# Bias tables without their zero columns and a landing margin for row products, in a one-core hybrid attention and state-space kernel

## The chip, the core and the metric

The kernel runs on one core of one Trainium2 chip. Its time is the device time of one execution in microseconds (us); lower is better. The time of a kernel is the median over several executions, and one further execution was recorded by the profiler. The engines are TensorE (PE; its weight loads are listed as PEld), VectorE (DVE), ScalarE (ACT), GpSimd (POOL) and SyncE (SP), which here only issues DMAs.

## The reference

Two layers are computed over 256 latent tokens (`x`, width 2048) with 256 context tokens. Each layer first makes a shift, a scale and a gate row from a conditioning vector by a vector-matrix product (`adaln`), normalizes and modulates the tokens, and adds the gated result of its mixer:

```python
for i in range(DEPTH):                      # 2 layers
    shift, scale, gate = adaln(c, ada_w[i], ada_b[i])     # silu(c) @ w + b, in three
    h = modulate(rms_norm(x, norm_g[i]), shift[:, None], scale[:, None])
    ...
    y = na_ssd_mixer(...) if i % 2 == 0 else short_conv_mixer(...)
    x = x + gate[:, None] * y
```

The first mixer has 16 neighbourhood-attention heads of width 128 and 32 state-space (SSD) heads behind one input projection, the second a gated short convolution. In an attention head the scores between the 256 latent queries (4 rows of 64) and the 256 latent keys get a bias that depends on the difference of row and column, and a mask that leaves 16 columns per query:

```python
bias = rpb[:, dr_idx[None, :, None], dc_idx[:, None, :]].reshape(nh, GRID_W, kh * GRID_W)
s_lat = jnp.einsum('bqhd,bkhd->bhqk', qr, kb).astype(jnp.float32) * scale + bias.astype(jnp.float32)
s_lat = jnp.where(mask, s_lat, -jnp.inf)
```

All is float32, and every large product is formed from three matmuls of split operands, described next.

## The kernel before

**Weights.** Each large weight comes from DRAM as pieces of 128 x 1024 floats (512 KB) into one of five buffers `raw` (L381 and L383, issued by SP). ACT rounds a piece to a short float (L420, the high half), DVE subtracts this from the piece (L427, the low half), and the two halves stand in one of three places `w0`, `w1`, `w2`. TensorE then forms high x high, high x low and low x high (L195). L427 is called a split below. A `raw` buffer is free again, and the next load into it can be issued, once its split has run. When three places are in use, a split waits until TensorE is done with the oldest.

**Stages.** After a start that makes the first layer's modulation, TensorE does the input projection for each of four groups of heads (to about 1100 us), then the output projection in three passes of columns, and then the second layer. Attention heads (`head_gen`) and SSD groups (`group_gen`) are done on DVE, ACT and TensorE beside the projections.

**What sets the order.** The work is written as generators in three queues: `urgent`, `side` (heads and groups) and `back`. A generator yields the engine it wants next, the tiles that must be ready, and how many PSUM banks it needs. A planner (class `Plan`) keeps a clock for each engine and for each tile, moved on by rough costs that are written in the kernel. The function `may` (L241) decides whether the next piece of a task is written now. For SP it asks that the tiles are ready by the planner's clock; for DVE and ACT that the engine's clock is within a horizon of TensorE's clock (`hor`: 4500, 2500 and 1500 ns for the three queues) and that the tiles are ready at most 400 ns from now. Once written, an instruction stands in its engine's queue for good: if its data comes later than planned, the engine waits there, and all that stands behind waits too.

**Row products.** The gate rows and the second layer's modulation need 2048 x 8192 weights (`adaT`). They are not multiplied by TensorE: the one task in `back` (`gemv_gen`) loads 128 pieces of 512 KB through the same `raw` buffers (L381) and multiplies and sums each on DVE with a broadcast row `csb` (L823, named CUSTOM_DVE_ANT_0 in the profile and ISA in the order of instructions). Results are first needed in the output projection, then in the second layer.

**Bias tables.** Two tiles `bias0` and `bias1` take turns over the 16 heads. For each head SP loads one table of 128 x 672 floats (336 KB, L1073) after the head two before has finished, DVE adds the mask in three places (L1078: columns 0 to 128, 304 to 368 and 544 to 672), and L1096 adds the table to the scores of each query half. The columns between are a gap of zeros that the table in DRAM holds.

**Other DVE work** named below: L1480 and L1483 scale an SSD group's output, L942 and L1613 make the low half of a mixed row, L1140 that of the attention weights, L571 and L989 normalize keys; L1456, L1461 and L1162 belong to SSD groups and heads.

Of the kernel before, what the change touches and what calls it, by code (L numbers as in the profile page):

```python
# [141 lines left out]
def kernel(ctx: ExitStack, tc, x, cx, ada0, w0, adaT, w_in, w_out, sc_in, sc_out, rpb, small, const,  # L142
# [7 lines left out]
    V, S, G, T, DMA = nc.vector, nc.scalar, nc.gpsimd, nc.tensor, nc.sync  # L150
    DMA2 = nc.scalar
    plan = Plan()
    E = plan.add

    def st(shape, tag, dt=F32, name=None):
        return sb.tile(list(shape), dt, tag=tag, name=name or tag, bufs=1)

    def drt(shape, name):
        return dr.tile(list(shape), F32, name="dram_" + name)
# [79 lines left out]
    def grow(task):  # L239
        _, t, h = task.cond  # L240
        if t - task.tmps > budget[0] or h - task.halves > budget[1]:  # L241
            return False
        cap(task, t, h)
        return True

    def may(task, hor, isurg):
        eng, aps, nb = task.cond
        if eng == "if":
            return aps()
        if eng == "grow":  # L250
            return grow(task)
        if nb and len(free_b) < nb + (0 if isurg else reserve[0]):
            return False
        if eng == "DVE":
            lows_try()
        now, t = plan.t["PE"], plan.t["ACT" if eng == "AQ" else eng]
        rdy = plan.ready(aps)
        if eng == "AQ":
            return t <= now + hor and rdy <= t
        if hor < 2000 and nb and sorted(plan.last[b.tensor.name] for b in free_b)[nb - 1] + 3000 > now:  # L260
            return False
        if hor < 2000:
            rdy += 4000 if eng == "PE" else 0
        if eng == "PE":
            if nb:
                rdy = max(rdy, sorted(plan.last[b.tensor.name] for b in free_b)[nb - 1])
            return rdy + (0 if isurg else 800) <= now + 100
        if eng == "SP":
            return rdy <= max(t, now) + 200
        return t <= now + hor and rdy <= max(t, now) + 400  # L270
# [7 lines left out]
    def pump():  # L278
        splits_try()
        again = True  # L280
        while again:
            again = False
            for q, hor in HOR[:2] if hold[0] else HOR:
                for task in list(q):
                    if not begin(task):
                        continue
                    if task.cond == "end":
                        sweep(q)
                        continue
                    if may(task, hor, q is urgent):  # L290
                        run(q, task)
                        if task.cond == "end":
                            sweep(q)
                        again = True
                        break
                if again:
                    break
# [134 lines left out]
    def lows_try():  # L432
        while lows and not hold[0] and plan.ready([lows[0][1]]) <= max(plan.t["PE"], plan.t["DVE"]) + 200:
            low_part()
# [340 lines left out]
    bias = [st([128, 3, 256], f"bias{k}") for k in range(2)]  # L775
# [149 lines left out]


    vd = drt([256, 512], "vd")
    dcol = P_("dcol")


# [136 lines left out]
    def head_gen(a, h):  # L1067
        hd = 4 * a + h
# [1 line left out]
        yield when(lambda: hd < 2 or ("pv", hd - 2) in got)  # L1070
        yield W_("SP")
        bf = bt.rearrange("p a b -> p (a b)")[:, :672]
        E(DMA.dma_start(bf, rpb[hd]))  # L1073
        yield W_("DVE", bt)
        for o_, m_ in ((0, mask[:, 0:32]), (304, mid), (544, mask[:, 32:64])):
            n_ = m_.shape[-1]
# [475 lines left out]
    for h in range(4):  # L1552
        spawn(side, head_gen(0, h))
# [11 lines left out]
    def do_qk(a, nxt):  # L1565
        psQ = banks(2)
        proj(512, "act", psQ, 4)
        spawn(urgent, kq_gen("Q", a, psQ, 2, statq, QT, QL, True), 2)
        psK = banks(4)
        proj(512, "act", psK, nxt)  # L1570
        spawn(urgent, kq_gen("K", a, psK, 4, statk, KT, KL, True), 4)
        for h in range(4 if a < 3 else 0):
            spawn(side, head_gen(a, h))
# [19 lines left out]
    for h in range(4):  # L1593
        spawn(side, head_gen(3, h))
# [516 lines left out]
```

## Time and profile before

| what | value |
|---|---|
| three timed executions | 1760.16, 1758.64, 1757.49 us (median 1758.64) |
| the profiled execution | 1761.34 us |
| its span, first to last instruction | 1759.6 us |
| PE busy / DVE busy / ACT busy / POOL busy | 1733.2 / 1218.6 / 768.1 / 31.4 us |
| mean granted TensorE clock | 0.999 |
| DMA | 381.86 MB, mean 217 GB/s |

In lines of groups the columns are: source line, engine, operation, tiles as out<-in with shapes, count, then busy time and the mean of one in ns, then the idle time of the engine just before such an instruction and what ended it. In lines of waits: how long in total, how many times, the longest. In rows of the timeline: start and duration in us, engine, line, and in brackets the idle time before and what released the instruction. In rows by stretch: the stretch, its length, each engine's busy time with its count, the granted clock, the share of DMA and GB/s.

### The profile page before, as it was taken

To read this page: it belongs to the slowest core of one execution; us is meant where nothing else is said; L and a number is where in the kernel's file an instruction comes from. 1 tells how busy PE (TensorE), PEld (TensorE's weight loads), DVE (VectorE), ACT (ScalarE), POOL (GpSimd) and SP (SyncE) were. 2 spreads that over 40 slices of the span, in tenths; PEclk is the share of its full clock that TensorE was granted. 3 is DMA by queue.
4 is the path that set the end of the run, shared out by engine and by line. 5 is a ranking of instruction groups with operands and counts; after the bars stand their busy time and mean duration, and the time that the engine had idled before them with its cause. 6 is when DMAs were issued, how large, how long until landed. Compare 5 with 4: busy or idle time off the path is not lost.

```text
span 1759.6 us, 25036 instructions
## 1 busy us (share of the span) xinstructions
PE 1733.2 (99%) x9451; PEld 1462.6 (83%) x9451; DVE 1218.6 (69%) x2042; ACT 768.1 (44%) x1330; POOL 31.4 (2%) x26
## 2 busy tenths in 40 slices
PE   6999999999999999999999999999999999999998
PEld 4777989888888888888888898888888888888887
DVE  5666777878476868676878687887668555555554
ACT  5333544446243436243436343664445444444432
POOL 0000100000000001000000000000000000000000
PEclk9999999999999999999999999999999999999999
DMA  9977644685765766665677567767867666666563
GB/s 368 347 295 258 206 150 150 201 241 190 231 198 158 239 190 209 207 220 171 212 219 219 180 213 239 242 227 266 290 218 251 208 187 192 191 191 191 190 205 120
DMA packets 188761, 381.86 MB, mean 217 GB/s; under 512 B 15536, under 2 KB 51168, under 8 KB 188640
## 3 DMA queue, kind: packets, MB, share of 16 engines
q1 hardware_dynamic: 181376, 373.68, 65.4%
q10 hardware_dynamic: 7264, 6.58, 1.1%
q8 instruction: 74, 1.21, 0.3%
q14 instruction: 47, 0.39, 0.1%
HBM read 372.71 MB, written 7.50 MB: 216 GB/s over the span
## 4 chain that ended last, share of the span: by engine, by line
PE 94%; DMA 2%; DVE 2%; ACT 1%; issue 0%; SPq 0%; POOL 0%; DVEq 0%; ACTq 0%
PE bank L195 90%; PE bank L199 3%; DMA tmp<-dram_csr 1%; DVE w L427 1%; DMA raw<-in_adaT 1%; DMA raw<-in_ada 0%; DVE raw L823 0%; DMA bias<-in_rpb 0%; ACT w L420 0%; DVE tmp L1456 0%; ACT tmp L1441 0%; DVE tmp L1445 0%; SPq L583 0%; ACT tmp L1451 0%; DVE tmp L759 0%
## 5 line engine op out<-in xcount | busy, mean ns | idle before, releaser
L420 ACT CAST w<-raw 128x1024 fp32r<-128x1024 f32 x343 | 359.1, 1049 | 519.9 <-PE bank L195 443.6
L427 DVE TENSOR_TENSOR w<-raw,w 128x1024 fp32r<-128x1024 f32 x343 | 416.5, 1218 | 232.9 <-ACT w L420 223.6
L195 PE MATMUL bank<-hH,w 128*128 128x256 f32 (+1 forms) x2064 | 488.4, 325 | 5.4 <-DVE w L427 5.4
L195 PE MATMUL bank<-w,hH 128*128 128x512 f32 x1280 | 406.3, 395 | 2.7 <-ACT hH L757 2.5
L195 PEld LDWEIGHTS bank<-hH,w 128*128 128x128 f32 x2064 | 345.7, 189 | 38.4 <-DVE w L427 6.6
L195 PE MATMUL bank<-hL,w 128*128 128x256 f32 (+1 forms) x1040 | 335.0, 322 | 0.0
L195 PEld LDWEIGHTS bank<-w,hH 128*128 128x128 f32 x1280 | 236.8, 188 | 54.1 <-issue 3.9
L195 PE MATMUL bank<-w,hL 128*128 128x512 f32 x640 | 249.5, 390 | 0.1
L195 PEld LDWEIGHTS bank<-hL,w 128*128 128x128 f32 x1040 | 197.0, 189 | 14.4
L195 PE MATMUL bank<-w,h 128*128 128x512 f32 x768 | 179.7, 390 | 0.0
L823 DVE CUSTOM_DVE_ANT_0 raw<-raw,csb 128x1024 f32<-128x1024 f32 x128 | 155.6, 1220 | 28.7 <-DMA raw<-in_adaT 23.0
L195 PEld LDWEIGHTS bank<-w,h 128*128 128x128 f32 x768 | 143.6, 188 | 29.6
L195 PEld LDWEIGHTS bank<-w,hL 128*128 128x128 f32 x640 | 120.1, 188 | 25.5 <-DVE hL L763 0.6
L195 PE MATMUL bank<-w,mix 128*128 128x512 f32 x588 | 138.6, 392 | 0.8 <-DVE w L427 0.8
L195 PEld LDWEIGHTS bank<-w,mix 128*128 128x128 f32 x588 | 109.3, 188 | 23.5 <-DVE w L427 1.7
L1276 DVE SCALAR_TENSOR_TENSOR tmp<-bank,cwh,tmp 128x508 f32<-128x508 f32 (+1 forms) x96 | 71.2, 745 | 1.8
L195 PE MATMUL bank<-KL,h 128*128 128x512 f32 x264 | 63.8, 389 | 0.0
L427 DVE TENSOR_TENSOR KL<-raw,KL 128x1024 fp32r<-128x1024 f32 x32 | 39.2, 1224 | 32.4 <-ACT KL L420 32.4
L427 DVE TENSOR_TENSOR QL<-raw,QT 128x1024 fp32r<-128x1024 f32 x32 | 39.2, 1224 | 29.4 <-ACT QT L420 29.3
L427 DVE TENSOR_TENSOR wL<-raw,wH 128x1024 fp32r<-128x1024 f32 x31 | 37.9, 1224 | 30.4 <-ACT wH L420 30.4
L195 PEld LDWEIGHTS bank<-KL,h 128*128 128x128 f32 x264 | 49.5, 188 | 10.2
L195 PE MATMUL bank<-QT,h 128*128 128x512 f32 x168 | 56.2, 391 | 0.0
(292 smaller groups left out, 1972.6 us busy)
## 6 DMA issues: line engine op xcount, KB each, us to landing
raw<-in_w_in SPq DMA_DIRECT2D x196, 512.0 KB, 3.8
raw<-in_adaT SPq DMA_DIRECT2D x128, 512.0 KB, 4.7
raw<-in_sc_in SPq DMA_DIRECT2D x128, 512.0 KB, 3.7
raw<-in_w_out SPq DMA_DIRECT2D x64, 512.0 KB, 4.9
raw<-in_ada SPq DMA_DIRECT2D x34, 512.0 KB, 6.7
raw<-in_sc_out SPq DMA_DIRECT2D x32, 512.0 KB, 3.6
PT<-in_ada SPq DMA_DIRECT2D x16, 512.0 KB, 6.9
raw<-in_w SPq DMA_DIRECT2D x16, 512.0 KB, 6.2
```

The source lines that it names most:

```text
L195: E(T.matmul(o, l, r, start=start, stop=stop, skip_group_check=True))
L199: E(T.transpose(o, i, ident if k == 128 else ident[:k, :k]))
L420: E(S.copy(H, v))
L427: E(V.tensor_tensor(out=Lo, in0=v, in1=H.bitcast(F32), op=ALU.subtract))
L823: E(V.tensor_tensor_reduce(out=raw, in0=raw, in1=csb, scale=1.0, scalar=0.0, op0=ALU.mult, op1=ALU.add, accum_out=gp[:, h, m:m + 1]))
L1276: E(V.scalar_tensor_tensor(out=do, in0=di, scalar=cwh[:, 32 * k + ch:32 * k + ch + 1], in1=do, op0=ALU.mult, op1=ALU.add))
```

## The change

1. The table in DRAM loses its gap: 320 columns per head in place of 672. SP loads it in three pieces (128, 64 and 128 columns: 64, 32 and 64 KB) into the same places of the tile. The zeros in between are written once, by POOL, into both tiles.
2. In `may`, a task of the queue `back` that wants DVE must have its tiles ready 2000 ns earlier by the planner's clock. Only the row products are in `back`.

```diff
@@ in may @@
         if hor < 2000:
-            rdy += 4000 if eng == "PE" else 0
+            rdy += 4000 if eng == "PE" else 2000 if eng == "DVE" else 0
@@ before the heads @@
+    for b_ in bias:
+        E(G.memset(b_.rearrange("p a b -> p (a b)")[:, 128:544], 0.0))
@@ in head_gen @@
         bf = bt.rearrange("p a b -> p (a b)")[:, :672]
-        E(DMA.dma_start(bf, rpb[hd]))
+        for o_, c_, n_ in ((0, 0, 128), (304, 128, 64), (544, 192, 128)):
+            E(DMA.dma_start(bf[:, o_:o_ + n_], rpb[hd, :, c_:c_ + n_]))
@@ in kernel(), on the host @@
-    gap = np.zeros((16, 128, 176), np.float32)
-    table = np.concatenate([pick(0, kc[:32]), gap, pick(0, kc[32:40]), pick(1, kc[24:32]), gap, pick(1, kc[32:])], axis=2)
+    table = np.concatenate([pick(0, kc[:32]), pick(0, kc[32:40]), pick(1, kc[24:32]), pick(1, kc[32:])], axis=2)
```

Lines behind the edits move by two or three: the mask's add is L1078 before and L1081 after, the table's load L1073 and L1076, and so on for all lines behind it.

Since the planner's clock decides what is written when, the order moves from the first row products on (about 170 us into the run). TensorE has the same instructions in another order; SP has 32 more DMAs, POOL two more instructions. The six row products that ran first stood ahead of the 35th split before; now 49 splits stand ahead of the sixth. The 64th stood behind 148 of DVE's 450 splits and now stands behind 162; the last behind 315, now 358. Three places follow, all on DVE.

**Place 1**, around a pair of tables whose load is issued at 402.56 us in the profile. `w0` to `w2` are weight places, `statk` belongs to the keys' norm, `half` and `yi` to an SSD group. Before:

```order
L1078 TENSOR_TENSOR bias0_159<-bias0_159,const_111 128x128
L1078 TENSOR_TENSOR bias1_160<-bias1_160,const_111 128x128
L1078 TENSOR_TENSOR bias1_160<-bias1_160,const_111 128x64
L1078 TENSOR_TENSOR bias1_160<-bias1_160,const_111 128x128
L427 TENSOR_TENSOR w2_97<-raw2_92,w2_97 128x1024
L823 ISA raw1_91,gp_167<-raw1_91,csb_166 128x1024
L823 ISA gp_167 128x1
L571 TENSOR_SCALAR statk_161<-statk_161 128x16
L1480 TENSOR_TENSOR half7_81<-bank7_89,yi_106 128x256
L1483 TENSOR_TENSOR half7_81<-half7_81,sz_104 128x256
L427 TENSOR_TENSOR w0_95<-raw0_90,w0_95 128x1024
```

Now:

```order
L1081 TENSOR_TENSOR bias0_159<-bias0_159,const_111 128x128
L1081 TENSOR_TENSOR bias1_160<-bias1_160,const_111 128x128
L1081 TENSOR_TENSOR bias1_160<-bias1_160,const_111 128x64
L1081 TENSOR_TENSOR bias1_160<-bias1_160,const_111 128x128
L823 ISA raw1_91,gp_167<-raw1_91,csb_166 128x1024
L823 ISA gp_167 128x1
L427 TENSOR_TENSOR w2_97<-raw2_92,w2_97 128x1024
L571 TENSOR_SCALAR statk_161<-statk_161 128x16
L427 TENSOR_TENSOR w0_95<-raw4_94,w0_95 128x1024
```

A row product has moved from behind the split of `w2` to ahead of it, and nothing long stands between the splits of `w2` and `w0` any more.

**Place 2**, around a later pair of tables, loaded from 669.56 us in the profile. Before:

```order
L1078 TENSOR_TENSOR bias1_160<-bias1_160,const_111 128x128
L1078 TENSOR_TENSOR bias1_160<-bias1_160,const_111 128x64
L1078 TENSOR_TENSOR bias1_160<-bias1_160,const_111 128x128
L823 ISA raw3_93,gp_167<-raw3_93,csb_166 128x1024
L823 ISA gp_167 128x1
L571 TENSOR_SCALAR statk_161<-statk_161 128x16
L427 TENSOR_TENSOR w0_95<-raw1_91,w0_95 128x1024
L427 TENSOR_TENSOR w1_96<-raw0_90,w1_96 128x1024
L427 TENSOR_TENSOR w2_97<-raw4_94,w2_97 128x1024
```

Now, from the row product ahead of the tables on:

```order
L823 ISA raw3_93,gp_167<-raw3_93,csb_166 128x1024
L823 ISA gp_167 128x1
L1081 TENSOR_TENSOR bias0_159<-bias0_159,const_111 128x128
L1081 TENSOR_TENSOR bias0_159<-bias0_159,const_111 128x64
L1081 TENSOR_TENSOR bias0_159<-bias0_159,const_111 128x128
L1081 TENSOR_TENSOR bias1_160<-bias1_160,const_111 128x128
L1081 TENSOR_TENSOR bias1_160<-bias1_160,const_111 128x64
L1081 TENSOR_TENSOR bias1_160<-bias1_160,const_111 128x128
L427 TENSOR_TENSOR w1_96<-raw4_94,w1_96 128x1024
L427 TENSOR_TENSOR w2_97<-raw2_92,w2_97 128x1024
L427 TENSOR_TENSOR w0_95<-raw1_91,w0_95 128x1024
```

Before, a split of `w1` and one of `w2` stood ahead of the tables, and a row product behind them and ahead of the next split of `w0`. Now the tables come ahead of those splits of `w1` and `w2`, a row product stands right ahead of the tables, and none between them and the split of `w0`.

**Place 3**, in the first pass of the output projection, ahead of the split that ends at about 1152.8 us in the profile; `mix` rows are the projection's other operand. Before:

```order
L823 ISA raw0_90,gp_167<-raw0_90,csb_166 128x1024
L823 ISA gp_167 128x1
L942 TENSOR_TENSOR mix12_9348<-half5_79,mix12_9348 128x256
L1140 TENSOR_TENSOR PL_2289<-bank2_84,PH_2288 128x4x128
L1140 TENSOR_TENSOR PL_2289<-bank7_89,PH_2288 128x4x128
L1613 TENSOR_TENSOR mix26_9361<-tmp2_67,mix26_9361 128x256
L427 TENSOR_TENSOR w0_95<-raw2_92,w0_95 128x1024
```

Now:

```order
L823 ISA raw2_92,gp_167<-raw2_92,csb_166 128x1024
L823 ISA gp_167 128x1
L427 TENSOR_TENSOR w0_95<-raw1_91,w0_95 128x1024
L427 TENSOR_TENSOR w1_96<-raw3_93,w1_96 128x1024
L1459 SCALAR_TENSOR_TENSOR tmp0_65<-tmp6_71,dtl_1622,tmp0_65 128x128 x2
L1464 TENSOR_TENSOR tmp3_68<-tmp0_65 128x256
L1165 TENSOR_TENSOR half2_76<-bank5_87,gt_101 128x256
L1143 TENSOR_TENSOR PL_2293<-bank4_86,PH_2292 128x4x128
```

The split of `w0` stands right behind the row product; the four instructions that stood between come later or elsewhere.

## The prediction

> **What bounds the kernel now.** The first part of the page gives each engine's busy time, and a line of its fifth part the row products:
>
> ```profile
> PE 1733.2 (99%) x9451; PEld 1462.6 (83%) x9451; DVE 1218.6 (69%) x2042; ACT 768.1 (44%) x1330; POOL 31.4 (2%) x26
> L823 DVE CUSTOM_DVE_ANT_0 raw<-raw,csb 128x1024 f32<-128x1024 f32 x128 | 155.6, 1220 | 28.7 <-DMA raw<-in_adaT 23.0
> ```
>
> PE is busy in 1733.2 of 1759.6 us and its matmuls stay the same, so whatever the change does to DVE, DMA or SP counts only where PE stands still for it. I therefore looked for PE's idle time, first by stretches:
>
> ```profile
> 0.00:38.00 38.00, 23.25 (x155) 15.64 (x156) 21.73 (x65) 23.15 (x50) 2.41 (x8) 1.00 0.96 375
> 400.00:415.00 15.00, 13.35 (x126) 12.48 (x123) 12.81 (x28) 10.86 (x43) 2.90 (x1) 1.00 0.57 186
> 660.00:705.00 45.00, 41.23 (x291) 38.25 (x291) 36.57 (x79) 26.85 (x78) 4.53 (x2) 0.96 0.64 205
> 1130.00:1180.00 50.00, 49.22 (x261) 41.06 (x260) 42.53 (x94) 29.44 (x61) 1.39 (x2) 1.00 0.71 236
> 1180.00:1754.00 574.00, 573.72 (x2590) 475.25 (x2589) 343.72 (x409) 253.96 (x311) 1.49 (x2) 1.00 0.65 210
> ```
>
> The start loses 14.75 us before any row product or table exists; the change leaves it alone but for two memsets. Between 38 and 1754 us three stretches hold the loss: 1.65, 3.77 and 0.78 us. The waits name one cause for it, and PE's timeline has the five places:
>
> ```profile
> PE bank L195 <- DVE w L427: 6.2, 5, 3.0
> 409.53 0.39 PE L195 MATMUL bank<-hH,w 128*128 128x256 f32 x1 [0.77 <-DVE w L427]
> 413.40 0.38 PE L195 MATMUL bank<-hH,w 128*128 128x256 f32 x1 [0.88 <-DVE w L427]
> 669.16 0.39 PE L195 MATMUL bank<-hH,w 128*128 128x256 f32 x1 [0.81 <-DVE w L427]
> 682.09 0.39 PE L195 MATMUL bank<-hH,w 128*128 128x256 f32 x1 [2.96 <-DVE w L427]
> 1152.85 0.50 PE L195 MATMUL bank<-w,mix 128*128 128x512 f32 x1 [0.78 <-DVE w L427]
> ```
>
> Each time a split came late: 0.77 + 0.88 + 0.81 + 2.96 + 0.78 = 6.20 us. The longest has a sequel, which the granted clock (third column from the right) shows in stretches of 2 us:
>
> ```profile
> 682.00:684.00 2.00, 1.91 (x14) 1.91 (x15) 2.00 (x3) 0.00 (x0) 2.00 (x1) 0.87 0.86 270
> 684.00:686.00 2.00, 2.00 (x12) 2.00 (x11) 1.50 (x3) 0.20 (x1) 0.79 (x1) 0.50 0.91 299
> 686.00:688.00 2.00, 2.00 (x15) 2.00 (x15) 2.00 (x4) 0.84 (x1) 0.00 (x0) 0.78 0.99 331
> 688.00:690.00 2.00, 2.00 (x20) 2.00 (x19) 1.48 (x3) 1.57 (x3) 0.00 (x0) 1.00 0.63 183
> ```
>
> After 2.96 us without work the clock fell: (0.13 + 0.50 + 0.22) x 2 = 1.70 us of work lost, though PE reads as busy. The four stalls under 0.9 us had no such sequel. The pool from which this change can gain is 6.20 + 1.70 = **7.90 us**.
>
> Why the splits were late stands in DVE's timeline:
>
> ```profile
> 406.83 0.63 DVE L1078 TENSOR_TENSOR bias<-bias,const 128x128 f32<-128x128 f32 x3 [1.11 <-DMA bias<-in_rpb]
> 407.70 0.63 DVE L1078 TENSOR_TENSOR bias<-bias,const 128x128 f32<-128x128 f32 x3 [0.24 <-DMA bias<-in_rpb]
> 408.25 1.22 DVE L427 TENSOR_TENSOR w<-raw,w 128x1024 fp32r<-128x1024 f32 x1
> 410.11 1.23 DVE L823 CUSTOM_DVE_ANT_0 raw<-raw,csb 128x1024 f32<-128x1024 f32 x1 [0.64 <-DMA raw<-in_adaT]
> ...
> 666.74 1.23 DVE L823 CUSTOM_DVE_ANT_0 raw<-raw,csb 128x1024 f32<-128x1024 f32 x1 [0.23 <-DMA raw<-in_adaT]
> ...
> 675.98 0.63 DVE L1078 TENSOR_TENSOR bias<-bias,const 128x128 f32<-128x128 f32 x3 [1.15 <-DMA bias<-in_rpb]
> 676.87 0.63 DVE L1078 TENSOR_TENSOR bias<-bias,const 128x128 f32<-128x128 f32 x3 [0.26 <-DMA bias<-in_rpb]
> 679.59 1.23 DVE L823 CUSTOM_DVE_ANT_0 raw<-raw,csb 128x1024 f32<-128x1024 f32 x1 [2.09 <-DMA raw<-in_adaT]
> 680.82 2.37 DVE L427 TENSOR_TENSOR w<-raw,w 128x1024 fp32r<-128x1024 f32 x2
> ```
>
> At 409 us the tables held DVE for 1.11 + 0.24 us right ahead of a split; at 413 and 669 us a row product stood ahead of one; at 682 us tables (1.15 + 0.26) and a row product (2.09) did so together. At 1152 us it was a row product and four short instructions.
>
> **The change part by part.** The profiled execution took 1761.34 us, 1.74 beyond its span, and lies 2.70 above the median of the timed runs, 1758.64. I add up against 1761.34 and take the 2.70 off at the end.
>
> *The margin.* In the new order a row product no longer stands between the tables and the split that was late at 682 us, none stands right ahead of the split at 669, and at 1152 the four short instructions are gone from between. These orders cover all five stalls, so the whole pool goes: **-7.90**. What takes their place is worked out next, from how the tables arrive.
>
> *The tables in three pieces.* These rows have SP's issues and how long they took to land:
>
> ```profile
> L1073 SPq DMA_DIRECT2D bias<-in_rpb x16: 422/461/944, 223.0 to 1159.8; - x16
> DMA to landing us min/median/max: 4.1/4.7/8.8
> 402.56 0.93 SPq L1073 DMA_DIRECT2D bias<-in_rpb  x2
> 662.26 1.33 SPq L1432 DMA_DIRECT2D tmp<-dram_csr  x2
> 669.56 0.94 SPq L1073 DMA_DIRECT2D bias<-in_rpb  x2
> tmp<-dram_exr SPq DMA_DIRECT2D x32, 128.0 KB, 5.3
> 673.32 0.28 PE L195 MATMUL bank<-hH,w 128*128 128x256 f32 x1
> ```
>
> A table of 336 KB lands in 4.7 us and a transfer of 128 KB in 5.3, so fewer bytes don't land sooner here; I give a piece the time t of a whole table, 4.1 to 8.8. Six issues in place of two at 0.46 us each put the last piece 4 x 0.46 = 1.85 later.
>
> Place 1: the issues stood behind the load that follows the split of w1, and stand ahead of both now, at least 1.22 + 0.37 = 1.59 sooner (split and issue) and, by their place among PE's matmuls in the new order, up to 2.7. The last piece goes out at 403.07 + 1.85 less 1.59 or 2.7, so at 403.3 or 402.2; I take 402.8. It lands at 402.8 + t; then come its add (0.28), now a row product (1.23 + 0.08) and the split of w2 (1.22): ready at 405.6 + t. PE ran out at 409.53 - 0.77 = 408.76. The stall is **t - 3.2**; with t = 4.7, the median, +1.5.
>
> Place 2: SP is free at 662.26 + 1.33 = 663.6, so the sixth issue starts near 666.0, where it stood at 670.1 (669.56 + 0.5). Add and split follow: ready at 667.5 + t. PE started on this w1 at 673.32, which is 672.5 without the stall at 669. The stall is **t - 5.0**. The tables here took 675.98 - 669.56 = 6.4 us, and I take the same: +1.4. Neither reaches 2.96, so I give neither a clock loss.
>
> [...]
>
> *Row products elsewhere.* They land later, the last behind 358 splits in place of 315. From 1180 us on about 12 more of them must run, 12 x 1.31 = 16 us, and DVE is busy there for 343.72 of 574, so this is hidden. Each holds its `raw` buffer some 2 us longer, and weight loads already wait for that:
>
> ```profile
> SPq L383 <- DVE gp L823: 68.0, 23, 6.9
> ACT w L420 <- DMA raw<-in_w_in: 17.8, 4, 4.7
> ```
>
> ACT absorbed these waits: none of PE's stalls names a DMA. Another order has other near misses, though; a new stall of the four small ones' kind is 0 to 0.88, and I take +0.4.
>
> *The memsets.* Two of 128 x 416 on POOL, at the start, ahead of everything that reads them:
>
> ```profile
> L517 DVE MEMSET cpad<- 128x512 f32 x1 | 0.5, 485 | 0.9 <-PEq L2100 0.9
> 36.22 0.55 POOL L572 TENSOR_TENSOR rx<-rx,const 128x1 f32<-128x1 f32 x1 [5.81 <-DVE rx L571]
> 36.80 0.88 DVE L615 TENSOR_SCALAR x<-x,rx 128x512 f32<-128x512 f32 x2 [0.66 <-POOL rx L572]
> 37.58 0.66 PE L199 MATMUL bank<-const,x 128*128 128x128 f32 x4 [0.29 <-ACT x L613]
> ```
>
> The order puts them behind this POOL instruction, with nothing long behind them on POOL. On DVE 512 columns take 0.485, so 416 would take about 0.4 (estimate); POOL's own price no row shows. If they disturb DVE beside them, x is at most 0.9 late for PE (the two L615); if not, 0. I take +0.4. Were they ahead of the POOL row, all of it would show, 0.8.
>
> Sum: -7.90 + 1.5 + 1.4 + 0.4 + 0.4 = **-4.2**: 1757.1 for a profiled execution, **1754.4** for the median.
>
> [...]
>
> **The rivals.**
>
> *The tables' landing takes the place of the row products' wait.* With t = 7 at both places: 3.8 with a clock loss of 1.7, and 2.0, with the small terms 0.8: -7.9 + 8.3 = +0.4, or 1759.0. For it: 6.4 at 669 us, and six issues that share DMA with weight loads. Against it: the median of 4.7. Chance 0.18.
>
> *Slower: both pairs at the longest landing.* t = 8.8 is in the row. Then 5.6 + 1.7 at place 1, 3.8 + 1.7 at place 2, 0.8 small: -7.9 + 13.6 = +5.7, or **1764.3**. It decides from 2t - 8.2 + 3.4 + 0.8 - 7.9 = 3.5, which is t = 7.7. For it: DVE takes its instructions in order, so one late piece of six is enough. Against it: 8.8 was the longest of 16. Chance 0.20.
>
> *The margin doesn't do what it says.* It is on the planner's clock, and a row product still waits 2.1 at place 1, now ahead of w2: 3.6 + 1.7 there, 1.4 at place 2, 0.81 + 0.78 left, 0.8 small: 9.1 - 7.9 = +1.2, or 1759.8. Chance 0.07.
>
> *Better.* With t = 4.1 place 1 keeps 0.9, place 2 nothing, and no small term comes: -7.0, or 1751.6. Chance 0.10.
>
> **How the numbers follow.** The forecast has 0.45, the rivals 0.18, 0.20, 0.07 and 0.10. What a measurement of this kernel tells from no change is about 0.2%, 3.5 us: faster is below 1755.1, slower above 1762.2. Of the forecast's 0.45 some 0.07 falls short of 3.5 us, so faster is 0.38 + 0.10 = 0.48, the same 0.07 + 0.18 + 0.07 = 0.32, slower 0.20. The range runs from 1750.5, the whole pool gone (7.9 off 1758.64, 1750.7), to 1762.5, between the first rival and the slow one, which is left out. The forecast's own range is 1751.5 to 1757.
>
> **What would show each step.** The wait of PE for L427 falls from 6.2 to about 3 us, with no row of 2.96 and the clock at 1.00 from 660 to 705. DVE's wait of 23.0 us for `adaT` falls to a few us. DVE's wait for tables rises, with stalls of PE right behind tables at about 409 and 672 us; if t is below 5 there are none. If PE stalls 0.5 or more at 37.6 us, the memsets cost. Wrong: PE stalls at a place that has neither a table nor a row product ahead of the late split, or PE waiting for a DMA through ACT.

## The result

The changed kernel takes 1753.22 us (median of 8 runs, 1752.37 to 1758.13). The kernel before takes 1760.26 us (8 runs, 1756.65 to 1764.07; the three runs shown at first are among them). The ratio is 0.9966, with a 95% interval of 0.9951 to 0.9981: faster by 0.34%. (The quotient of the two medians alone would be 0.9960.)

The profiled execution took 1752.57 us and its span is 1750.8, which is 8.8 less than before. These are the stretches and the waits that answer to those of before:

```profile
0.00:38.00 38.00, 23.10 (x153) 15.55 (x154) 21.82 (x65) 22.95 (x50) 3.19 (x10) 1.00 0.96 374
400.00:415.00 15.00, 15.00 (x131) 14.95 (x130) 10.42 (x22) 10.29 (x40) 4.50 (x2) 1.00 0.81 254
660.00:705.00 45.00, 45.00 (x334) 41.32 (x333) 35.08 (x79) 26.83 (x73) 3.70 (x2) 1.00 0.55 166
1130.00:1180.00 50.00, 50.00 (x266) 42.34 (x265) 41.61 (x93) 29.65 (x57) 1.39 (x2) 1.00 0.70 228
...
DVE raw L823 <- DMA raw<-in_adaT: 10.0, 10, 2.7
...
DVE bias L1081 <- DMA bias<-in_rpb: 3.0, 5, 1.3
```

PE is busy all through the three stretches that lost 1.65, 3.77 and 0.78 us, and the clock is 1.00. PE's waits for L427 are gone. Row products wait 10.0 us for their weights, 23.0 before; the tables hold DVE as long as before, 3.0 us for 3.1. So the whole pool of 7.90 us went.

At place 1 DVE waits for PE ahead of the tables, and each piece has landed when its add comes up; at place 2 the tables cost 1.32 us, and no split is late for it:

```profile
404.66 0.87 DVE L1516 SCALAR_TENSOR_TENSOR half<-half,small,bank 128x256 f32<-128x256 f32 x2 [2.53 <-PE bank L199]
405.45 1.16 DVE L1081 TENSOR_TENSOR bias<-bias,const 128x128 f32<-128x128 f32 x6
...
667.00 1.37 DVE L1081 TENSOR_TENSOR bias<-bias,const 128x128 f32<-128x128 f32 x6 [1.32 <-DMA bias<-in_rpb]
```

### The profile page after: what moved, and what is told of

Same layout as the page of the kernel before. It is cut to its first block, busy times and chain, and to the rows that moved or that the text cites. A ratio compares the mean times of both kernels' runs of the same rounds, so it can differ in the third digit from the quotient of the medians.

```text
span 1750.8 us, 25076 instructions
## 1 busy us (share of the span) xinstructions
PE 1730.9 (99%) x9451; PEld 1461.3 (83%) x9451; DVE 1218.1 (70%) x2042; ACT 768.5 (44%) x1330; POOL 33.2 (2%) x28
## 4 chain that ended last, share of the span: by engine, by line
PE 98%; DMA 0%; DVE 0%; SPq 0%; ACT 0%; issue 0%; POOL 0%; DVEq 0%; ACTq 0%
PE bank L195 95%; PE bank L199 3%; DMA raw<-in_ada 0%; SPq L583 0%; DVE w L427 0%; DVE tmp L603 0%; DVE tmp L759 0%; ACT half L724 0%; ACT x L613 0%; DVE tmp L2016 0%; DVE tmp L2018 0%; DVE hL L763 0%; SPq L381 0%; ACT hH L757 0%; DVE gt L789 0%
## 5 line engine op out<-in xcount | busy, mean ns | idle before, releaser
L427 DVE TENSOR_TENSOR w<-raw,w 128x1024 fp32r<-128x1024 f32 x343 | 416.4, 1217 | 260.6 <-ACT w L420 254.7
L427 DVE TENSOR_TENSOR QL<-raw,QT 128x1024 fp32r<-128x1024 f32 x32 | 39.2, 1224 | 29.0 <-ACT QT L420 28.9
L427 DVE TENSOR_TENSOR KL<-raw,KL 128x1024 fp32r<-128x1024 f32 x32 | 39.2, 1224 | 28.4 <-ACT KL L420 28.3
L427 DVE TENSOR_TENSOR wL<-raw,wH 128x1024 fp32r<-128x1024 f32 x31 | 37.9, 1224 | 27.4 <-ACT wH L420 27.4
```

Of the source, the lines that this page charges most:

```text
L427: E(V.tensor_tensor(out=Lo, in0=v, in1=H.bitcast(F32), op=ALU.subtract))
```

## The experiments

All were timed over five rounds beside the kernel before; tables_only has 5 runs, margin_from_640 6, the others 11 or 12. The orders of instructions can be held fixed here: in six kernels the planner is fed the costs of one form of the tables (`plan.slot`, which books the DMAs and issues none) while the DMAs issued have another form. PE, DVE and ACT then have row for row the order named.

### The two parts, apart and crossed

**margin_only**: the line in `may` alone, tables whole.

> The margin of 2000 ns alone, tables loaded whole. Theory A (the order that the margin makes takes the row products' waits out from ahead of the late splits, and the tables matter little): PE's wait for L427 falls from 6.2 to under 2 us, DVE's wait for adaT from 23 to about 10, ratio to before 0.9955 to 0.998. Theory B (the tables land sooner in pieces, and that is the gain): DVE still waits for tables ahead of a split, PE's wait for L427 stays at 4 to 7 us, ratio 0.999 to 1.001. Theory C (any other order would do, the one before was an unlucky draw): no link between the wait for adaT and the stalls, ratio 0.996 to 1.000.

**tables_only**: the changed kernel without that line.

> The tables in three pieces alone, margin 0. Theory A: row products still wait 15 to 25 us for adaT, and PE's wait for L427 stays between 4 and 8 us, ratio 0.999 to 1.001. Theory B: both the tables' wait and PE's wait for L427 fall under 2 us, ratio 0.9955 to 0.998. Theory C: the order changes too (160 of DVE's rows), so PE's wait falls to under 2 us with adaT waits as long as before, ratio 0.996 to 0.998.

**whole_in_after_order**: the changed kernel's order, but

```diff
-        for o_, c_, n_ in ((0, 0, 128), (304, 128, 64), (544, 192, 128)):
-            E(DMA.dma_start(bf[:, o_:o_ + n_], rpb[hd, :, c_:c_ + n_]))
+        DMA.dma_start(bf, rpb[hd])
+        for o_, n_ in ((0, 128), (304, 64), (544, 128)): plan.slot(512 * n_, [bf[:, o_:o_ + n_]])
```

> Every instruction of PE, DVE, ACT and POOL in exactly the order of the changed kernel, but each table loaded whole by one DMA of 336 KB. Theory A: ratio 0.9955 to 0.998 as the changed kernel, landing back at a median of 4.7 us in place of 3.6, DVE's wait for tables between 2 and 5 us, PE's wait for L427 0 to 1. Theory B: tables hold up splits again, PE waits 2 us or more for L427, ratio 0.998 to 1.000.

**pieces_in_before_order**: the order of the kernel before, but

```diff
-        E(DMA.dma_start(bf, rpb[hd]))
+        plan.slot(512 * 672, [bf])
+        for o_, c_, n_ in ((0, 0, 128), (304, 128, 64), (544, 192, 128)): DMA.dma_start(bf[:, o_:o_ + n_], rpb[hd, :, c_:c_ + n_])
```

> Every instruction of PE, DVE and ACT in exactly the order of the kernel before, but each table loaded in three pieces and the gap set by POOL. Theory A: the row products' waits stay, PE's wait for L427 5 to 8 us (last piece goes out 1.85 us later and lands about 1.1 sooner), ratio 0.9995 to 1.0015. Theory B: DVE's wait for tables falls from 3.1 to under 1 us and PE's wait for L427 to 2 to 4 us, ratio 0.997 to 0.999.

Measured: margin_only 0.9998 (0.9989 to 1.0007), tables_only 1.0034 (1.0022 to 1.0047), whole_in_after_order 1.0002 (0.9991 to 1.0012), pieces_in_before_order 1.0013 (1.0003 to 1.0023). Neither part gains anything alone, and with the order held fixed the pieces are worth about 0.36% in the new order (1.0002 against 0.9966) and nothing in the old one, where they cost 0.13%. Theory A, that of the prediction, falls: it gave the gain to the margin. B falls too, since tables_only is slower, at a ratio that no theory had in its range. Single expectations held: A's for pieces_in_before_order (PE waits 6.75 us for L427, ratio 1.0013) and B's for PE's wait in whole_in_after_order (4.20 us). C is tested below.

These are DVE's rows ahead of the stall at place 2, first with whole tables in the new order, then with pieces in the old:

```profile
667.58 1.22 DVE L823 CUSTOM_DVE_ANT_0 raw<-raw,csb 128x1024 f32<-128x1024 f32 x1
668.73 0.08 DVE L823 DVE_READ_ACCUMULATOR2_ANT gp<- 128x1 f32 x1
673.94 0.63 DVE L1081 TENSOR_TENSOR bias<-bias,const 128x128 f32<-128x128 f32 x3 [5.13 <-DMA bias<-in_rpb]
674.81 0.63 DVE L1081 TENSOR_TENSOR bias<-bias,const 128x128 f32<-128x128 f32 x3 [0.24 <-DMA bias<-in_rpb]
675.36 3.49 DVE L427 TENSOR_TENSOR w<-raw,w 128x1024 fp32r<-128x1024 f32 x3
```

```profile
676.82 1.16 DVE L1081 TENSOR_TENSOR bias<-bias,const 128x128 f32<-128x128 f32 x6
681.92 1.22 DVE L823 CUSTOM_DVE_ANT_0 raw<-raw,csb 128x1024 f32<-128x1024 f32 x1 [3.94 <-DMA raw<-in_adaT]
683.07 0.08 DVE L823 DVE_READ_ACCUMULATOR2_ANT gp<- 128x1 f32 x1
683.07 0.17 DVE L571 TENSOR_SCALAR statk<-statk 128x16 f32<-128x16 f32 x1
683.15 3.50 DVE L427 TENSOR_TENSOR w<-raw,w 128x1024 fp32r<-128x1024 f32 x3
```

In the first the row product no longer waits, and a table does, for 5.13 us. In the second the tables are in, and the row product behind them waits 3.94 us, longer than the 2.09 of before. Each part takes away one of two waits on the way to the same split, and the other fills the time. This is the first rival of the prediction (the tables' landing takes the place of the row products' wait), and it is what margin_only does: DVE waits 6.08 us there for one table.

The stalls of PE at the two places, one row each with the clock's sequel worked out as before, in these two kernels:

```profile
412.34 0.50 PE L195 MATMUL bank<-hH,w 128*128 128x256 f32 x2 [1.76 <-DVE w L427]
676.63 0.50 PE L195 MATMUL bank<-hH,w 128*128 128x256 f32 x2 [2.44 <-DVE w L427]
```

```profile
412.34 0.50 PE L195 MATMUL bank<-hH,w 128*128 128x256 f32 x2 [2.48 <-DVE w L427]
684.42 0.80 PE L195 MATMUL bank<-hH,w 128*128 128x256 f32 x2 [3.49 <-DVE w L427]
```

The 1.76 had no fall of the clock behind it, 2.44 and 2.48 had one of 1.70 us of work each (stretches of 2 us with 0.52 and 0.63 of the clock, and with 0.89, 0.50 and 0.76), 3.49 one of 3.40. The last section sets the gaps and the falls side by side.

### Why a whole table lands late in the new order

At place 2 the two tables land like this, whole in the new order, and in pieces in the changed kernel (issues of L1435 load the `csr` rows of an SSD group, two transfers ahead of the tables):

```profile
663.95 0.97 SPq L1435 DMA_DIRECT2D tmp<-dram_csr  x2
664.97 0.95 SPq L1075 DMA_DIRECT2D bias<-in_rpb  x2
666.90 0.38 SPq L383 DMA_DIRECT2D raw<-in_w_in  x1
...
DMA to landing us min/median/max: 9.0/9.1/9.3
```

```profile
660.21 0.97 SPq L1435 DMA_DIRECT2D tmp<-dram_csr  x2
661.23 2.87 SPq L1076 DMA_DIRECT2D bias<-in_rpb  x6
666.29 0.38 SPq L383 DMA_DIRECT2D raw<-in_w_in  x1
...
SPq L383 <- DMA tmp<-dram_csr: 1.8, 1, 1.8
...
DMA to landing us min/median/max: 4.3/5.1/5.8
```

Whole, the second table lands 9.3 us after its own issue near 665.5, which is 9.8 us after the first issue of the pair. In pieces the last lands 4.3 us after its issue near 663.8, 6.8 after the first issue, though it goes out later. The tables land in the order of issue, right behind the second `csr` transfer: 0.9 and 1.7 us behind it when whole, 0.2 to 1.3 us in pieces. So of the 3.0 us between the two kernels 2.5 us is the landing of that `csr` transfer (8.6 us after its issue, 6.1 in the changed kernel), and only 0.5 is the tables' own.

This also tells what the new order changed for a whole table. In the order before, the `csr` loads went out 7.3 us ahead of the tables (662.26 and 669.56 us) and had landed at 668.68 and 669.34; in the new one the tables go out right behind them.

Two causes for the sooner landing in pieces are open: fewer bytes (320 KB for 672 a pair), or the number of DMAs. The wait row shows a way for the latter: the weight load behind six pieces had to wait 1.8 us for the landing of the first `csr` transfer, which is the eighth DMA ahead of it; behind two whole tables the first `csr` is only the fourth ahead, and the load waits for no `csr` transfer (it waits 1.2 us for DVE's L1483). While it waits, one load of 512 KB less is under way beside the tables. Why it waits for that landing, no run shows.

**three_with_gap**: the new order, three DMAs that carry the gap too.

```diff
+        [DMA.dma_start(bf[:, i:j], rpb[hd, :, i:j]) for i, j in ((0, 304), (304, 544), (544, 672))]
```

> PE, DVE, ACT and POOL in exactly the order of the changed kernel; each table still comes by three DMAs, but these carry the gap too (152, 120 and 64 KB, 336 KB in all). Theory D1 (a table lands sooner because it has 160 KB in place of 336): at the pair around 665 us it lands 8 to 9.5 us after its first issue as when loaded whole, PE waits 2 to 4 us for L427 in all, ratio 0.999 to 1.001. Theory D2 (it lands sooner because more DMAs are in flight and take a larger share of the engines from the other transfers): it lands 5 to 6.5 us after its first issue, no wait of PE for L427, ratio 0.996 to 0.9975.

**one_strided**: the new order, one DMA of three runs of 128 columns, 192 KB.

```diff
+        DMA.dma_start(bass.AP(tensor=bf.tensor, offset=bf.offset, ap=[bf.ap[0], [272, 3], [1, 128]]), rpb[hd].rearrange("p (c n) -> p c n", c=3))
```

> The same order of PE, DVE, ACT and POOL; each table comes by one DMA with three runs of 128 columns (192 KB, most of the gap left out). Theory D1 (bytes): at about 665 us it lands within 6.5 us of its issue and PE waits under 1 us for L427, ratio 0.996 to 0.9975. Theory D2 (number of DMAs): it lands 8 to 9.5 us after its issue, PE waits 2 to 4 us, ratio 0.999 to 1.001.

**whole_and_two_small**: the new order, a whole table and two DMAs of 8 KB behind it.

```diff
+        [DMA.dma_start(*x) for x in ((bf, rpb[hd]), *((bt.rearrange("p a b -> p (a b)")[:, k:k + 16], rpb[hd, :, :16]) for k in (704, 736)))]
```

> The changed kernel's order of PE, DVE, ACT and POOL; each table whole by one DMA of 336 KB, and behind it two DMAs of 8 KB into columns that nothing reads, so that a pair of tables is six DMAs with 688 KB. Theory E (six DMAs in a row fill the places for DMAs in flight, the weight load behind them waits for an earlier transfer to land, and meanwhile the tables have the DMA engines to themselves): at about 665 us the load behind is issued only when the first csr transfer has landed, 2 us or more after the last of the six; the pair lands 7.5 to 8.8 us after its first issue in place of 9.8; PE waits 1 to 2.5 us for L427 and keeps its clock, ratio 0.998 to 0.9993. Theory F (only bytes count): the pair lands after 9.5 to 10.5 us, PE waits 4 us or more, ratio 0.9998 to 1.001.

**two_dmas**: the new order, 160 KB in two DMAs.

```diff
+        DMA.dma_start(bass.AP(tensor=bf.tensor, offset=bf.offset, ap=[bf.ap[0], [544, 2], [1, 128]]), rpb[hd, :, :256].rearrange("p (c n) -> p c n", c=2)), DMA.dma_start(bf[:, 304:368], rpb[hd, :, 256:])
```

> The same order again; each table's 160 KB by two DMAs (128 KB in two runs of 128 columns, and 32 KB), so a pair is four DMAs. Theory E: four don't fill the places, the load behind goes out as soon as its buffer is free, and the pair lands 7.8 to 8.8 us after its first issue as with one strided DMA each, ratio 0.9975 to 0.9985. Theory F: it lands after 6.5 to 7.2 us as in the changed kernel, with no wait of PE over 0.7 us, ratio 0.9962 to 0.9975.

Measured at place 2, each from the issues and landings of one profiled execution. (Two further executions with the changed kernel's tables there, in changed_again and margin_from_640, have 7.1 and 6.8 us for the pair, so some 0.3 us is spread.) The load behind counts from the issue of the second `csr` transfer, the pair from its own first issue:

| kernel | KB a pair, DMAs | load behind issued | second csr lands | pair lands | ratio to before |
|---|---|---|---|---|---|
| margin_only | 672, 2 | 1.7 us | 8.8 us | 10.0 us | 0.9998 (0.9989 to 1.0007) |
| whole_in_after_order | 672, 2 | 2.4 | 8.6 | 9.8 | 1.0002 (0.9991 to 1.0012) |
| one_strided | 384, 2 | 3.2 | 8.1 | 8.8 | 0.9982 (0.9971 to 0.9993) |
| two_dmas | 320, 4 | 3.4 | 7.1 | 7.7 | 0.9975 (0.9966 to 0.9985) |
| whole_and_two_small | 688, 6 | 5.8 | 7.0 | 8.7 | 0.9985 (0.9974 to 0.9996) |
| three_with_gap | 672, 6 | 5.7 | 6.8 | 8.3 | 0.9979 (0.9969 to 0.9988) |
| changed kernel | 320, 6 | 5.6 | 6.1 | 6.8 | 0.9966 (0.9951 to 0.9981) |

Both causes hold, and neither alone. Fewer bytes in two DMAs bring 1.0 us at this place and in four DMAs 2.1, six DMAs with all the bytes 1.1 to 1.5, both together 3.0. In the four kernels with two or four DMAs, two loads of 512 KB go out before the second `csr` transfer has landed, in the three with six DMAs only one. That these loads are what holds the `csr` transfer up is argued, since the number of DMAs changes along with them.

None of the four theories held as written. D1 expected 8 to 9.5 us of three_with_gap and met 8.3, but not its wait of PE for L427 (2 to 4 us; 1.3 was found) nor its ratio; of D2 the landing of one_strided came (8.8 us for 8 to 9.5), not its ratio. F expected 9.5 to 10.5 us of whole_and_two_small and 6.5 to 7.2 of two_dmas, and 8.7 and 7.7 were found. E expected 7.5 to 8.8 and a ratio of 0.998 to 0.9993 for whole_and_two_small and met both, but not its wait of PE (1 to 2.5 us; 0.43 was found), and the load behind came late mostly because the six issues themselves took 4.58 us; of two_dmas it expected 7.8 to 8.8 us, and 7.7 was found. That there are places for DMAs in flight which six of them fill, as E supposes, no run shows; the runs show the load behind waiting for a `csr` landing, 1.8 us in the changed kernel and 0.3 us in whole_and_two_small, and for none in whole_in_after_order and two_dmas. In whole_and_two_small:

```profile
661.65 4.58 SPq L1075 DMA_DIRECT2D bias<-in_rpb  x6
666.96 0.38 SPq L383 DMA_DIRECT2D raw<-in_w_in  x1
...
SPq L383 <- DMA tmp<-dram_csr: 0.3, 1, 0.3
```

That two DMAs of 8 KB added to a whole table make the kernel faster (0.9985 against 1.0002) can have nothing to do with bytes saved. The two intervals overlap by a little (0.9991 to 0.9996), so this step is less sure than the others.

### Is it the order, or any other order?

**margin_4000** and **margin_1000**: the changed kernel with other margins.

> The changed kernel with a margin of 4000 ns in place of 2000; PE, DVE and ACT take another order from 170 us on. If the margin works by keeping row products from waiting: DVE's wait for adaT falls from 10.0 to under 6 us, no wait of PE for L427 over 1 us, ratio 0.9955 to 0.9975. If the order of 2000 is a lucky draw among orders: PE waits 1 to 6 us for L427 at some other place, ratio 0.998 to 1.001.

> The changed kernel with a margin of 1000 ns. If the margin works by its size: DVE's wait for adaT between 12 and 20 us (10.0 at 2000, 25.5 at 0), PE's wait for L427 between 1 and 6 us, ratio 0.998 to 1.001. If any other order than that of margin 0 would do: ratio 0.9965 to 0.998 with any wait for adaT.

**margin_from_640**: pieces_in_before_order, with the margin only late in the run.

```diff
-            rdy += 4000 if eng == "PE" else 0
+            rdy += 4000 if eng == "PE" else 2000 * (now > 640000) if eng == "DVE" else 0
```

> Tables in three pieces; the order of PE, DVE and ACT is that of the kernel before up to 640 us of the planner's clock, and the margin of 2000 ns holds only from there, so that place 2 has the changed kernel's order and place 1 that of before. If the account by places is right: the stall at 412 us of the order of before with pieces stays (2.48 us, 1.70 of clock), those at 684 us (3.49 and 3.40 of clock) go, in all 6 to 7 us less of loss than there, ratio 0.9970 to 0.9990 to the kernel before. If any other order would do: stalls at other places, no link to place 2.

**changed_again**: the changed kernel, beside three_with_gap, one_strided and margin_4000.

> The changed kernel once more, on the chip of the three others: ratio 0.9955 to 0.998 by every theory, no stall of PE over 0.5 us between 50 and 1740 us.

Measured, with the waits of DVE's row products for `adaT`:

| margin | adaT wait | ratio to before |
|---|---|---|
| 0 (tables_only) | 25.5 us | 1.0034 (1.0022 to 1.0047) |
| 1000 | 15.1 | 1.0006 (0.9998 to 1.0015) |
| 2000, changed kernel | 10.0 | 0.9966 (0.9951 to 0.9981) |
| 2000, changed_again | 11.4 | 0.9969 (0.9960 to 0.9979) |
| 4000 | 0.6 | 0.9977 (0.9968 to 0.9986) |

With the pieces in place the time follows the row products' wait down to 2000, in orders that differ in hundreds of rows. That speaks against a lucky order (theory C). 4000 takes away nearly all of the wait and brings no more: its ratio lies just outside the 0.9955 to 0.9975 that was expected. In changed_again one stall of 0.61 us was found where none over 0.5 was expected.

margin_from_640 is 0.9972 (0.9961 to 0.9983). The stall at place 1 stays and that at place 2 is gone, as expected; the one at place 1 is the only one over 0.3 us after 100 us. Against pieces_in_before_order 8.5 us of loss went by the account below, where 6 to 7 were expected, since the stall at place 1 is shorter and the small one near 1156 us went too:

```profile
411.28 0.50 PE L195 MATMUL bank<-hH,w 128*128 128x256 f32 x2 [1.85 <-DVE w L427]
```

### The account over all kernels

For each profiled execution: PE's idle gaps over 0.1 us between 100 and 1740 us, what the clock lost there in stretches of 2 us (1 minus the granted clock, times 2), and the span less both.

| kernel | gaps | clock | span | span less both |
|---|---|---|---|---|
| before | 6.5 | 1.7 | 1759.6 | 1751.4 |
| changed | 0.0 | 0.0 | 1750.8 | 1750.8 |
| changed_again | 0.6 | 0.0 | 1752.2 | 1751.6 |
| margin_only | 4.8 | 1.7 | 1757.8 | 1751.3 |
| tables_only | 8.9 | 5.1 | 1764.7 | 1750.7 |
| whole_in_after_order | 5.4 | 1.7 | 1758.8 | 1751.7 |
| pieces_in_before_order | 7.0 | 5.1 | 1762.7 | 1750.6 |
| three_with_gap | 3.1 | 0.0 | 1753.9 | 1750.8 |
| one_strided | 1.0 | 0.0 | 1752.5 | 1751.5 |
| whole_and_two_small | 0.8 | 0.0 | 1751.5 | 1750.7 |
| two_dmas | 2.5 | 1.7 | 1754.9 | 1750.7 |
| margin_from_640 | 1.9 | 1.7 | 1753.6 | 1750.0 |
| margin_1000 | 4.8 | 0.0 | 1756.7 | 1751.9 |
| margin_4000 | 1.3 | 0.0 | 1753.5 | 1752.2 |

The last column lies within 1.1 us of 1751.1 for all fourteen while the spans differ by 13.9. So the stalls and their sequels in the clock tell the spans apart to about 1 us, and the changed kernel's profiled execution has none left to lose. No kernel here beats it.

Some spread remains that isn't told by the order. In the new order PE waits at about 396 us for L1464, behind a late `csr` landing: 0 in the changed kernel, 0.61 in changed_again, 1.72 in three_with_gap, and in two_dmas

```profile
398.01 0.90 PE L195 MATMUL bank<-tmp,xtm 128*64 128x128 f32 x5 [2.46 <-DVE tmp L1464]
```

with 1.70 us of clock behind it, 4.2 in all. Two of the 8 runs of the changed kernel, 1757.15 and 1758.13, lie about that much above the others; that they had this stall is argued, since they have no trace.

## Why the prediction was right, and where it was not

The forecast of 1754.4 and its direction were right; the reasons were right only in part, and the closeness of the number (1753.22) is in part luck. The forecast was a gain of 4.2 us on three runs with a median of 1758.64; the eight runs of that kernel have 1760.26, from which the same gain gives 1756.1. The medians lie 7.0 us apart. By its gain and by its reason, a short t, this is the rival *Better* (-7.0), which was given 0.10.

1. **The pool, -7.90.** Right in size and place. All five stalls went and the clock stayed at 1.00. That the new order alone would keep it was wrong: with whole tables in that order PE waits 4.20 us for L427 and the clock loses 1.70, and with the margin alone the ratio is 0.9998.
2. **"Fewer bytes don't land sooner here; I give a piece the time t of a whole table."** This is the step that failed. The last piece landed in 2.8 us at place 1 and 4.3 at place 2, where 4.7 and 6.4 were taken. The prediction compared transfers of different streams at different moments. In the same order and place, the whole table took 6.9 and 9.3.

   The path of the sum around t held. With t = 2.8 and 4.3 its forms t - 3.2 and t - 5.0 give no stall. With 6.9 and 9.3, less the 1.85 us by which the last of two issues is ahead of the last of six, they give 1.85 and 2.45; whole_in_after_order has 1.76 and 2.44 (at place 2 two differences of about 0.3 us cancel).
3. **Place 1, +1.5.** Measured 0. The tables' landing lay under DVE's wait of 2.53 us for PE, which the sum didn't have. The split ended 0.21 us before PE needed it, so with t = 4.7 there would have been a stall.
4. **Place 2, +1.4.** Measured 0. DVE waited 1.32 us for the tables, and the split still ended 1.55 us before PE needed it.
5. **New small stalls, +0.4.** Measured 0 in the profiled execution, 0.6 in changed_again.
6. **The memsets, +0.4.** Measured 0.04. They run beside the two L615, which took 1.41 us here and 0.88 before, but PE waits 0.33 where it was 0.29:

```profile
L929 POOL MEMSET bias<- x2: 446/446/446, 36.9 to 37.3; 128x416 f32 x2
...
37.01 1.41 DVE L615 TENSOR_SCALAR x<-x,rx 128x512 f32<-128x512 f32 x2 [0.66 <-POOL rx L572]
...
37.79 0.87 PE L199 MATMUL bank<-const,x 128*128 128x128 f32 x6 [0.33 <-ACT x L613]
```

7. **Row products later, at no cost.** Right. From 1180 to 1745 us DVE is busy for 353.27 us where it was 342.33, and PE is busy in 565.00 of 565:

```profile
1180.00:1745.00 565.00, 565.00 (x2552) 468.13 (x2551) 353.27 (x427) 249.91 (x306) 1.49 (x2) 1.00 0.69 221
```

The four terms given back, 3.7 us in all, were each too large; so the profiled execution gained 8.8 us where 4.2 was forecast. Beyond the pool it gained a gap of 0.28 us at 1309 us that the pool leaves out, and 0.6 us that no gap and no clock row shows.

Of the signs named, PE's wait for L427 fell further than to 3 us, and DVE's wait for tables didn't rise (3.0 us for 3.1).

The first rival, the tables' landing in place of the row products' wait, was given 1759.0. It didn't come, and margin_only and whole_in_after_order show that only the pieces kept it away: 9.3 us of landing at place 2, or 7.5 counted from where the last of six would go out, is beyond the 7 of this rival and near the 7.7 from which the slow one was to decide. The third rival (the margin doesn't do what it says) is out: the wait for adaT fell to 10.0.

At place 2 a pair of tables in pieces of 32 and 64 KB landed sooner (6.8 us after its first issue) than one in two DMAs of 336 KB (9.8), and sooner than one in two of 192 KB (8.8).

On the clock, the prediction gave no loss to stalls shorter than 2.96 us. Shorter gaps had one too: that of 1.85 us in margin_from_640 had 1.70 us of lost work behind it. One of 2.03 in margin_1000 had none.

## What to carry to other kernels

Where two waits stand in a row ahead of the same split, the removal of one shows nothing until the other goes too; try both parts together, and cross them, before one of them is dropped. When the order of a kernel hangs on a planner, hold the order fixed and change the transfer alone: that told the pieces' worth, which neither part by itself did. How long a transfer took to land moved here with its place and with what was issued around it, more than with its own bytes: of the 3.0 us that the pieces bring at place 2, 2.5 are the landing of the transfer ahead.

## What the runs showed of the hardware

- The same transfer landed at different times after its issue. The second `csr` transfer, the same 256 KB each time, landed 8.8, 8.6, 8.1 and 7.1 us after its issue where the next weight load went out 1.7, 2.4, 3.2 and 3.4 us behind it, and 6.1 to 7.0 where it went out 5.6 to 5.8 behind (the tables between them differ in bytes and in the number of DMAs too, so that no run changes the load's time alone).
- The issue of a table's DMA by SP took 0.43 us at the median in the kernels with six a pair. At place 2 one of the six took 1.37 us in three_with_gap and one 1.57 in whole_and_two_small, with large tables under way ahead of it; in the changed kernel none there took over 0.47.
- In each fall between 100 and 1740 us the clock stood at 0.50 for 3.41 us (before: 683.48 to 686.90), which is 1.70 us of lost work, or for twice that. These rows of pieces_in_before_order hold one fall of the first kind, of which only the first row is shown, and one of the second; a fall starts before the end of its first row by twice what that row has lost:

```profile
412.00:414.00 2.00, 1.66 (x12) 1.67 (x13) 1.97 (x6) 0.00 (x0) 0.41 (x1) 0.89 0.27 35
...
682.00:684.00 2.00, 0.00 (x0) 0.00 (x0) 2.00 (x4) 0.88 (x3) 0.69 (x1) 0.80 0.03 12
684.00:686.00 2.00, 1.58 (x7) 1.58 (x8) 2.00 (x3) 0.00 (x0) 2.00 (x1) 0.50 0.80 221
686.00:688.00 2.00, 2.00 (x11) 2.00 (x10) 1.50 (x3) 0.00 (x0) 1.12 (x1) 0.50 0.89 266
688.00:690.00 2.00, 2.00 (x11) 2.00 (x11) 1.63 (x3) 0.69 (x1) 0.00 (x0) 0.50 1.05 344
```

The longer one lost (0.20 + 0.50 + 0.50 + 0.50) x 2 = 3.40 us. About 0.6 us of it, half of the 1.22 from the fall's start to PE's next matmul at 684.42, lies beside idle time, so that the account of this kernel is that much too high; in tables_only it is 1.1.

The starts are 413.56 and 683.20 us, and the distance, 269.64, is 79 times the 3.413 us that the fall in before lasted. Two other executions have two falls each: in before at 683.48 and 1758.68 us, 315 times 3.413 apart, in tables_only at 412.72 and 685.80, 80 times.

In the 3.41 us ahead of each fall between 100 and 1740 us PE had been idle for at least 1.85 us (margin_from_640, a gap to 411.28 and a fall from 411.96) and at most all of the 3.41 (tables_only, a gap from 409.30 to 413.13 and a fall from 412.72). The longest gaps with no fall behind them are 1.72 us (three_with_gap), 1.76 (whole_in_after_order) and 2.03 (margin_1000). So the length of a gap alone doesn't sort them, and what does, no run shows. In the two falls of double length PE was still idle for 1.22 us (pieces_in_before_order) and 2.24 us (tables_only) after the start; in margin_only it was for 0.53 us, and that fall was a single one.
